# Hybrid decoder trunk on one core: operand sums emitted two FFN tiles early, four FFN weights split through a DMA, residual additions at the norm's priority

## The chip, the cores and the metric

One core of one Trainium2 chip runs the whole program. The metric is the device time of one execution in microseconds, here the median of three runs. A separate profiled execution gives the trace; its own time stands in the table below.

## The reference, cut to what matters

Two layers on 528 tokens (16 meta tokens and 512 of input) of width 1024, all float32. Each layer is a token mixer and a gated MLP, each behind an RMSNorm and with a plain residual add; a last RMSNorm follows. The change touches the MLP and the norms:

```python
def conv_glu_ffn(h, w_up, conv_w, conv_b, w_down):
    u = causal_dwconv(jnp.einsum('btd,df->btf', h, w_up), conv_w, conv_b)
    gate, val = jnp.split(u, 2, axis=-1)
    return jnp.einsum('btf,fd->btd', jax.nn.silu(gate) * val, w_down)
...
for l in range(DEPTH):
    h = h + hybrid_mixer(rmsnorm(h, norm_mix_g[l]), w_in[l], ...)
    h = h + conv_glu_ffn(rmsnorm(h, norm_ffn_g[l]), w_up[l], ..., w_down[l])
return rmsnorm(h, final_norm_g)[:, N_META:]
```

D_FF is 2816, so the MLP has 22 tiles of 128 hidden units, each with a gate and a value.

## The kernel before

**Products in three terms.** Every large float32 product is taken with operands split into a high part and a remainder: weight wh and wl, activation xh and xl. One 128x128 block is three matmuls: wh by xh, wh by xl, wl by xh (`product`, and `q` in `pair_products`). The activations lie transposed, features on the partitions and tokens on the columns; the 528 columns are worked in two halves of 264 (256 or 258 where the last layer drops the meta tokens).

**How a split is made.** `split` (L420 to L427) casts the high part on ScalarE (L421). The remainder is one subtraction on VectorE (L427), or, with `by_dma=True`, a negated copy on ScalarE (L424) and a DMA from the GpSimd queue that adds the source to it (L425). Before, the second way is used for the down-projection weights `rd` that are spread into the FFN tiles, and for the sums `th`, `tl`.

**Weights.** `raw_src` lists the weight tiles in the order of their use and `items` says how each is prepared: "p" is a split on VectorE, "q" a split through the DMA, "a" to "d" make the sums that a fast tile needs. `take` (where TensorE picks up an item) prepares three items ahead by `prep`. Weights land in three buffers `raw`, by DMAs from the SyncE queue, and the split parts in four buffers each of `wh` and `wl`. An up-projection tile is 128x1024.

**FFN tiles.** Tiles 0 to 3 and 21 are plain: gate and value, two halves each, 8 blocks of three matmuls a half (`up_pair`). Tiles 4 to 20 are fast (`up_fast`): gate and value share seven products of half the size in place of eight (`pair_products`), which needs sums and differences of blocks of the weights and of the normalised activations. In a fast tile the order on TensorE is: products on X_B11 and X_B21, then X_T1 and X_T2, two half products of the down projection of the four tiles before, X_B22 and X_T3, two more down halves, X_T4. Each of the seven is 12 matmuls, a half of the down projection too. T1 to T4 are the operand sums, made once a layer by `sum_pair(a)` for each of four pairs of feature blocks: two additions that put xh and xl together (L1049), four additions and subtractions (L1055 to L1060), and two splits by DMA into `th` and `tl`. A pair takes four work buffers `t`, and the buffers that hold its results are free again when the DMAs have read them. Tile u and convolution buffers come out of the same seven buffers `t` (`TM = 7`): four for an FFN tile. In the loop over `GROUPS` near the end of `layer`, `sum_pair` is emitted behind plain tiles 1, 2 and 3.

**Order of the work.** TensorE and the SyncE queue run in the order in which the code emits. VectorE, ScalarE and GpSimd are ordered when the program is built, by a list scheduler with a model of time: of what is ready there, the instruction emitted first goes first, and `tc.high_priority(n)` lets its block go as if it had been emitted n places earlier. Norm generators (`norm_rest`, `norm_split`) run under `URGENT['n']` = 400 from `tick`. The residual additions and squares of `resid_sq` (L979, and L437, L441, L442 in `norm_sq`) have no such priority before.

Of the kernel before, what the change touches and what calls it, by code (L numbers as in the profile page):

```python
# [13 lines left out]
ALU = mybir.AluOpType  # L14
# [5 lines left out]
KD = D // P  # L20
SEQ = 512
META = 16
T = SEQ + META
# [7 lines left out]
NFF = 22  # L31

GROUPS = ((0, 4), (4, 8), (8, 12), (12, 16), (16, 22))
FAST = range(4, 21)
DOWNS = ((), (2, 2, 2, 2), (2, 2, 2, 2), (2, 2, 2, 2), (2, 2, 2, 1, 1, 0))
TM = 7
Q0 = 12
MAXH = 2
# [5 lines left out]
URGENT = {'h': 400, 'r': 400, 'n': 400, 'f': 400}  # L44
# [49 lines left out]
def hybrid_trunk_kernel(ctx, tc, x, w_in, w_out, w_up, w_down, par, pre_in, lru_w, kon, msk, rope, out):  # L94
    nc = tc.nc
    V, S, G, PE = nc.vector, nc.scalar, nc.gpsimd, nc.tensor
# [23 lines left out]
    def half(tag="hs", bufs=4):  # L120
        return tpool.tile([P, 264], F32, tag=tag, name=nm(tag), bufs=bufs)
# [49 lines left out]
    hT = const.tile([P, KD, T], F32, tag="hT", name="hT")  # L171
# [28 lines left out]
    raw_src, items = [], []  # L200
# [4 lines left out]
        group[f"x{j}"], group[f"y{j}"], group[f"s{j}"] = [M_LX + j], [M_LY + j], [M_RG + j]  # L205
    orders = [[m for k in o.split() for m in group[k]] for o in (ORDER, ORDER1)]

    def plain(src, kn, ring="raw"):
        raw_src.append((src, kn, ring))
        items.append(("p" if ring == "raw" else "q", len(raw_src) - 1, kn))  # L210

    for l in range(DEPTH):
        for m in orders[l]:
            plain(w_in[l, m], KD)
        for m in range(KD):
            plain(w_out[l, m], KD)

        for g, (k0, k1) in enumerate(GROUPS):
            rows = iter(range(KD))
            for i, j in enumerate(range(k0, k1)):  # L220
                down = [next(rows) for _ in range(DOWNS[g][i] if g else 0)]
                if j in FAST:
                    raw_src.extend((w_up[l, r], KD, "raw") for r in (j, NFF + j))
                    ri = len(raw_src) - 2
                    items.extend((k, ri, KD) for k in "ab")
                    for q, m in enumerate(down):
                        plain(w_down[l, m, :, slice(*GROUPS[g - 1]), :], 4, "rd")
                        if q == 0:
                            items.append(("c", ri, KD))
                    if not down:  # L230
                        items.append(("c", ri, KD))
                    items.append(("d", ri, KD))
                else:
                    plain(w_up[l, j], KD)
                    plain(w_up[l, NFF + j], KD)
        for m in range(KD):
            plain(w_down[l, m, :, k0:k1, :], k1 - k0)
    raws, ready, sums = {}, {}, {}
# [193 lines left out]
    def norm_sq(k, t0, n, apart=False):  # L432

        if k == 0 or apart and k == KD - 1:
            a = half("acc", 3) if k == 0 else half("hs")
            accs.setdefault(t0, []).append(a)
            S.activation(a[:, 0:n], hT[:, k, t0:t0 + n], AF.Square)  # L437
            return
        a = accs[t0][0]
        sq = half("hs")  # L440
        S.activation(sq[:, 0:n], hT[:, k, t0:t0 + n], AF.Square)  # L441
        V.tensor_tensor(a[:, 0:n], a[:, 0:n], sq[:, 0:n], op=ALU.add)  # L442
# [52 lines left out]
    def whole(hi, lo):  # L495
        return lambda t0, n: (hi[:, t0:t0 + n], lo[:, t0:t0 + n])
# [406 lines left out]
    def layer(l):  # L903
# [72 lines left out]

        def resid_sq(m):
            def f(i, t0, n, ps):
                V.tensor_tensor(hT[:, m, t0:t0 + n], hT[:, m, t0:t0 + n], ps[:, 0:n], op=ALU.add)  # L979
                norm_sq(m, t0, n, t0 + n == T)  # L980
            return f

        def norm_next(blk, hi_):
# [6 lines left out]
        phase[0].release()  # L990
        phase[0], n_t[0] = tc.alloc_tile_pool(name=f"mlp{l}", bufs=1), TM
        c0 = META if lastl else 0
# [33 lines left out]
        def up_pair(j):  # L1026
            us = {}

            def ev(key, m):

                def f(i, t0, n, ps):
                    if key not in us:
                        us[key] = new_u()
                    u, c = us[key]
                    S.copy(u[:, 2 + t0:2 + t0 + n], ps[:, 0:n])
                    o = max(t0, c0)
                    tap(u, c, m, o, t0 + n, ps[:, o - t0:n])
                return f
            return [(None, ev("g", j), lambda: gate(j, us)), (None, ev("v", NFF + j), lambda: value(j, us))]
# [4 lines left out]
        def sum_pair(a):  # L1044

            y = []
            for k in (2 * a, 2 * a + 1):
                y.append(big())
                V.tensor_tensor(y[-1][:, 0:2 * hn], xh[:, k, h0:T].bitcast(F32), xl[:, k, h0:T].bitcast(F32), op=ALU.add)  # L1049
            (b11, b12), (b21, b22) = ((t[:, 0:hn], t[:, hn:2 * hn]) for t in y)  # L1050
            for i in (0, 2):
                t = big()
                p0, p1 = t[:, 0:hn], t[:, hn:2 * hn]
                if i == 0:
                    V.tensor_tensor(p0, b11, b12, op=ALU.subtract)  # L1055
                    V.scalar_tensor_tensor(p1, p0, -1.0, b22, op0=ALU.mult, op1=ALU.subtract)
                    t2 = p1
                else:
                    V.tensor_tensor(p0, b22, b12, op=ALU.subtract)
                    V.scalar_tensor_tensor(p1, t2, -1.0, b21, op0=ALU.mult, op1=ALU.subtract)  # L1060
                split(t[:, 0:2 * hn].rearrange("p (h t) -> p h t", t=hn), *(x[:, a, i:i + 2, 0:hn] for x in tsum),
                      by_dma=True)
# [7 lines left out]
        def up_fast(j, halves):  # L1070
            us = {k: new_u() for k in "gv"}
            ug, uv = (us[k][0][:, 2 + h0:2 + T] for k in "gv")

            def evac(what, ps):
                p = ps[:, 0:hn]
                if what == "c11":
                    S.copy(ug[:, 0:hn], p)
                elif what == "u":
                    S.copy(ug[:, hn:2 * hn], p)
                elif what == "q5":  # L1080
                    S.activation(uv[:, hn:2 * hn], p, AF.Copy, scale=-1.0)
                elif what == "c11b":
                    V.tensor_tensor(ug[:, 0:hn], ug[:, 0:hn], p, op=ALU.add)
                elif what == "c12":
                    V.tensor_tensor(ug[:, hn:2 * hn], ug[:, hn:2 * hn], p, op=ALU.add)  # L1085
                    u, c = us["g"]
                    tap(u, c, j, c0, T, u[:, 2 + c0:2 + T])
                    gate(j, us)
                elif what == "v":
                    V.tensor_tensor(uv[:, hn:2 * hn], uv[:, hn:2 * hn], p, op=ALU.subtract)  # L1090
                else:
                    S.activation(uv[:, 0:hn], p, AF.Copy, scale=-1.0)
                    u, c = us["v"]
                    tap(u, c, NFF + j, c0, T, u[:, 2 + c0:2 + T])
                    value(j, us)
            cut_at = (len(halves) + 1) // 2

            def between(i):
                for f in (halves[:cut_at], halves[cut_at:])[i]:
                    f()  # L1100
            pair_products(xs_fast, KD // 2, hn, evac, between)

        def down_halves(m, xs):

            w = []

            def f(t0, n):
                if not w:
                    w.append(take())
                ps = ps_mm.tile([P, 512], F32, tag="mm", name=nm("mm"))  # L1110
                product(w[0], xs, t0, n, range(len(xs)), ps, True, True)
                resid(m)(0, t0, n, ps)
            return [lambda t0=t0, n=n: f(t0, n) for t0, n in hd]

        for g, (k0, k1) in enumerate(GROUPS):
            rows = iter(range(KD))
            prev = [whole(*act[k]) for k in range(*GROUPS[g - 1])] if g else []
            for i, j in enumerate(range(k0, k1)):
                halves = [f for _ in range(DOWNS[g][i] if g else 0) for f in down_halves(next(rows), prev)]
                if j in FAST:  # L1120
                    up_fast(j, halves)
                else:
                    if j == 0:
                        run_units([u for i_ in range(2) for u in up_pair(i_)], xs_norm, hv, first=4)
                    elif j > 1:
                        run_units(up_pair(j), xs_norm, hv)
                    if j in (1, 2, 3):
                        for a in {1: (0,), 2: (1, 2), 3: (3,)}[j]:
                            sum_pair(a)

        def final(t0, n):
# [27 lines left out]
    with tc.manual_schedule(engines={mybir.EngineType.PE, mybir.EngineType.SP}):  # L1159
# [132 lines left out]
        for l in range(DEPTH):  # L1292
            layer(l)
# [106 lines left out]
```

## Time and profile before

| what | us |
|---|---|
| median of 3 runs | 1287.32 (1286.71 to 1287.97) |
| the profiled execution, its own time | 1288.41 |
| span of its trace | 1286.5 |
| TensorE busy / VectorE busy / ScalarE busy | 1258.5 / 988.6 / 752.0 |
| mean granted TensorE clock | 0.987 |

A row of the trace gives an engine, a line of the kernel, the operation and its tiles (out<-in, buffer numbers left out); "idle before" or the bracket at the end is the time that the engine stood before it and what ended that. The engines are PE (TensorE), DVE (VectorE), ACT (ScalarE), POOL (GpSimd) and SP (SyncE); a q behind a name is the queue of that engine. Times are counted from the start of the span.

### The profile page before, as it was taken

The page shows a single profiled execution, that of the slowest core. Times are in us where ns is not written, and L with a number is a line of the kernel's source. Part 1 is how long each engine was busy: PE and PEld are TensorE (multiplying, and loading weights), DVE is VectorE, ACT ScalarE, POOL GpSimd, SP SyncE. Part 2 cuts the span into 40 slices and gives each one's busy share as a digit, 9 for nine tenths or more (in the row PEclk, how much of TensorE's full clock was granted, in tenths as well). Part 3 has the DMA queues.
Part 4 walks back from the last instruction along what each step waited for, and adds up shares of the span by engine and source line. Part 5 has one row for each costly group of instructions (what it writes and reads, how often), then busy time and mean ns, then how long its engine had stood idle before and what let it go on. Part 6 is the DMA issues. An engine that isn't in the chain of part 4 may idle for free.

```text
span 1286.5 us, 25758 instructions
## 1 busy us (share of the span) xinstructions
PE 1258.5 (98%) x10244; PEld 1245.9 (97%) x10244; DVE 988.6 (77%) x1946; ACT 752.0 (58%) x1442; POOL 79.5 (6%) x179
## 2 busy tenths in 40 slices
PE   9999999999899999999999999999999999999997
PEld 8999999999899999999999999999989999999996
DVE  7987676468788888887588767764896888888865
ACT  6665555347666666666456645553684666666652
POOL 0000000001211111100000000000021111111000
PEclk8999999999899999999999999999998999999998
DMA  5322312324555445544232223122265555555422
GB/s 197 98 78 67 100 50 66 99 67 122 126 132 132 131 128 136 132 124 115 75 99 67 66 66 100 50 83 66 87 136 139 132 132 131 132 137 135 111 88 74
DMA packets 53240, 135.32 MB, mean 105 GB/s; under 512 B 5632, under 2 KB 12288, under 8 KB 53120
## 3 DMA queue, kind: packets, MB, share of 16 engines
q1 hardware_dynamic: 39424, 110.46, 27.5%
q0 software_dynamic: 12544, 21.06, 9.7%
q10 hardware_dynamic: 1152, 2.16, 0.5%
q8 instruction: 80, 1.31, 0.4%
q14 instruction: 40, 0.33, 0.1%
HBM read 110.51 MB, written 2.10 MB: 88 GB/s over the span
## 4 chain that ended last, share of the span: by engine, by line
PE 86%; DVE 6%; ACT 3%; DMA 3%; issue 1%; SPq 0%; POOL 0%; DVEq 0%; ACTq 0%; POOLq 0%
PE mm L130 63%; PE mx L130 23%; DMA tl<-t 2%; DVE t L1000 1%; PE mx L137 1%; DVE wl L427 1%; DVE t L567 1%; DVE t L1138 0%; DMA raw<-in_w_in_dram 0%; DVE sc L591 0%; ACT wh L421 0%; ACT th L421 0%; DMA mk<-in_msk_dram 0%; DVE t L870 0%; ACT sc L674 0%
## 5 line engine op out<-in xcount | busy, mean ns | idle before, releaser
L130 PE MATMUL mm<-xh,wh 128*128 128x264 f32 (+1 forms) x1424 | 417.9, 293 | 0.8 <-ACT xh L421 0.8
L130 PE MATMUL mm<-xl,wh 128*128 128x264 f32 (+1 forms) x1424 | 404.3, 284 | 0.7 <-DVE xl L427 0.3
L130 PE MATMUL mm<-xh,wl 128*128 128x264 f32 (+1 forms) x1424 | 403.4, 283 | 0.0
L130 PE MATMUL mm<-ah,wh 128*128 128x264 f32 (+2 forms) x960 | 273.2, 285 | 0.0
L130 PEld LDWEIGHTS mm<-xl,wh 128*128 128x128 f32 x1424 | 268.8, 189 | 3.7 <-issue 1.9
L130 PE MATMUL mm<-al,wh 128*128 128x264 f32 (+2 forms) x960 | 272.4, 284 | 0.0
L130 PE MATMUL mm<-ah,wl 128*128 128x264 f32 (+2 forms) x960 | 272.1, 283 | 0.0
L130 PEld LDWEIGHTS mm<-xh,wh 128*128 128x128 f32 x1424 | 268.5, 189 | 3.6 <-issue 2.0
L130 PEld LDWEIGHTS mm<-xh,wl 128*128 128x128 f32 x1424 | 268.6, 189 | 0.2 <-DVE wl L1195 0.2
L427 DVE TENSOR_TENSOR wl<-raw,wh 128x1024 fp32r<-128x1024 f32 (+2 forms) x168 | 182.5, 1088 | 82.2 <-ACT wh L421 81.7
L421 ACT CAST wh<-raw 128x1024 fp32r<-128x1024 f32 (+2 forms) x168 | 158.3, 942 | 149.2 <-PE mm L130 143.6
L130 PEld LDWEIGHTS mm<-ah,wh 128*128 128x128 f32 x960 | 182.0, 190 | 0.1
L130 PEld LDWEIGHTS mm<-al,wh 128*128 128x128 f32 x960 | 181.9, 189 | 0.1
L130 PEld LDWEIGHTS mm<-ah,wl 128*128 128x128 f32 x960 | 181.9, 189 | 0.0
L1000 DVE SCALAR_TENSOR_TENSOR t<-t,pr,t 128x528 f32<-128x528 f32 (+1 forms) x176 | 132.7, 757 | 11.1 <-ACT t L1005 5.1
L130 PE MATMUL mx<-th,wh 128*128 128x264 f32 (+1 forms) x408 | 117.2, 287 | 0.0
L130 PE MATMUL mx<-th,wl 128*128 128x264 f32 (+1 forms) x408 | 116.6, 286 | 0.0
L130 PE MATMUL mx<-tl,wh 128*128 128x264 f32 (+1 forms) x408 | 116.3, 285 | 0.0
L1005 ACT ACTIVATE t<-t,pr 128x528 f32<-128x528 f32 (+1 forms) x68 | 56.0, 823 | 58.5 <-DVE t L1085 56.5
L427 DVE TENSOR_TENSOR wl<-ss,wh 128x1024 fp32r<-128x1024 f32 x68 | 83.0, 1221 | 4.6 <-ACT wh L421 1.8
L425 POOL DMA_DIRECT2D wl<-rd x64 | 56.6, 884 | 448.6 <-ACT wl L424 384.4
L130 PEld LDWEIGHTS mx<-tl,wh 128*128 128x128 f32 x408 | 78.3, 192 | 0.0
(231 smaller groups left out, 2170.9 us busy)
## 6 DMA issues: line engine op xcount, KB each, us to landing
raw<-in_w_up_dram SPq DMA_DIRECT2D x88, 512.0 KB, 3.6
raw<-in_w_in_dram SPq DMA_DIRECT2D x52, 512.0 KB, 3.6
rd<-in_w_down_dram SPq DMA_DIRECT2D x64, 256.0 KB, 2.7
wl<-rd POOLq DMA_DIRECT2D x64, 256.0 KB, 3.6
raw<-in_w_out_dram SPq DMA_DIRECT2D x16, 512.0 KB, 3.5
raw<-in_w_down_dram SPq DMA_DIRECT2D x16, 384.0 KB, 3.1
hT<-in_x_dram SPq DMA_DIRECT2D x4, 528.0 KB, 5.4
t<-in_rope_dram ACTq DMA_DIRECT2D x8, 264.0 KB, 3.3
```

Of the source, the lines that this page charges most:

```text
L130: PE.matmul(o, a, b, start=start, stop=stop, **kw)
L137: PE.transpose(o, a, ident[0:n, 0:n])
L421: S.copy(hi, src)
L425: G.dma_start(lo, src, accum_op=ALU.add)
L427: V.tensor_tensor(lo, src, hi.bitcast(F32), op=ALU.subtract)
L567: V.tensor_tensor(o, a, b, op=ALU.mult)
L1000: V.scalar_tensor_tensor(c[:, 0:cn], u[:, i + c0:i + c0 + cn], pr[l][:, w + i:w + i + 1], c[:, 0:cn], op0=ALU.mult, op1=ALU.add)
L1005: S.activation(c[:, a - c0:b - c0], src, AF.Identity, bias=pr[l][:, C_FB + m:C_FB + m + 1], scale=pr[l][:, C_FW + 3 * m + 2:C_FW + 3 * m + 3])
```

## The change

Three edits. The gate and value weights of FFN tiles 2 and 3 are split through the DMA in place of VectorE. The four `sum_pair` calls come behind tiles 1 and 2, two behind each, in place of one, two and one behind tiles 1, 2 and 3. The residual addition, its square and the running sum of squares get the priority that the norm has.

```diff
+SENT = (2, 3)
...
-    def plain(src, kn, ring="raw"):
+    def plain(src, kn, ring="raw", by_dma=False):
         raw_src.append((src, kn, ring))
-        items.append(("p" if ring == "raw" else "q", len(raw_src) - 1, kn))
+        items.append(("q" if by_dma else "p", len(raw_src) - 1, kn))
...
-                        plain(w_down[l, m, :, slice(*GROUPS[g - 1]), :], 4, "rd")
+                        plain(w_down[l, m, :, slice(*GROUPS[g - 1]), :], 4, "rd", True)
...
-                    plain(w_up[l, j], KD)
-                    plain(w_up[l, NFF + j], KD)
+                    plain(w_up[l, j], KD, by_dma=j in SENT)
+                    plain(w_up[l, NFF + j], KD, by_dma=j in SENT)
...
         def resid_sq(m):
             def f(i, t0, n, ps):
-                V.tensor_tensor(hT[:, m, t0:t0 + n], hT[:, m, t0:t0 + n], ps[:, 0:n], op=ALU.add)
-                norm_sq(m, t0, n, t0 + n == T)
+                with tc.high_priority(URGENT['n']):
+                    V.tensor_tensor(hT[:, m, t0:t0 + n], hT[:, m, t0:t0 + n], ps[:, 0:n], op=ALU.add)
+                    norm_sq(m, t0, n, t0 + n == T)
...
-                    if j in (1, 2, 3):
-                        for a in {1: (0,), 2: (1, 2), 3: (3,)}[j]:
+                    if j in (1, 2):
+                        for a in {1: (0, 1), 2: (2, 3)}[j]:
                             sum_pair(a)
```

## Rows read from the trace of the kernel before

**Rows 1.** The page: busy us, share of the span and instructions of each engine.
```profile
PE 1258.5 (98%) x10244; PEld 1245.9 (97%) x10244; DVE 988.6 (77%) x1946; ACT 752.0 (58%) x1442; POOL 79.5 (6%) x179
```

**Rows 2.** What TensorE waited for in the whole span: us in total, times, longest.
```profile
PE mm L130 <- DMA tl<-t: 9.0, 2, 4.8
PE mm L130 <- ACT th L421: 2.5, 2, 1.5
PE mx L130 <- DVE acc L442: 2.0, 2, 1.2
```

**Rows 3.** Fast tiles 4, 5 (layers 0, 1): us; PE, PEld, DVE, ACT, POOL busy; PEclk; DMA.
```profile
324.19:348.34 24.15, 18.88 (x134) 18.46 (x133) 16.76 (x29) 14.12 (x26) 4.73 (x8) 0.86 0.60 133
348.34:364.38 16.04, 16.04 (x134) 16.04 (x133) 13.66 (x22) 10.03 (x16) 1.85 (x4) 1.00 0.50 132
957.23:982.47 25.24, 19.00 (x134) 18.59 (x133) 16.86 (x30) 14.33 (x26) 6.18 (x6) 0.80 0.64 128
982.47:998.20 15.73, 15.73 (x135) 15.73 (x133) 13.26 (x22) 9.96 (x16) 1.71 (x2) 1.00 0.50 135
```

**Rows 4.** The chain that ended last, layer 0, around tile 4: start, us, what.
```profile
330.23 3.75 DMA tl<-t
...
334.03 0.81 PE mm L130 x2
```

**Rows 5.** Busy time by stretch (columns as in rows 3): plain tiles before tile 4.
```profile
293.30:324.19 30.89, 30.89 (x258) 30.89 (x256) 30.41 (x48) 24.21 (x46) 4.64 (x9) 1.00 0.55 138
...
927.00:957.23 30.23, 30.23 (x255) 30.23 (x255) 29.75 (x48) 23.60 (x45) 5.23 (x5) 1.00 0.59 139
```

**Rows 6.** Groups by line and shape, 293.3 to 324.19 us, VectorE and ScalarE: busy us, mean ns.
```profile
L427 DVE TENSOR_TENSOR wl<-raw,wh 128x1024 fp32r<-128x1024 f32 x5 | 6.1, 1216 | 2.6 <-ACT wh L421 2.6
L1049 DVE TENSOR_TENSOR t<-xh,xl 128x528 f32<-128x528 f32 x6 | 4.1, 696 | 0.1
...
L1055 DVE TENSOR_TENSOR t<-t 128x264 f32<-128x264 f32 x3 | 1.3, 418 | 0.0
...
L421 ACT CAST wh<-raw 128x1024 fp32r<-128x1024 f32 x4 | 4.2, 1050 | 1.1 <-PE mm L130 1.1
```

**Rows 7.** VectorE in order of time, layer 0: start us, us, what.
```profile
322.91 0.41 DVE L1060 SCALAR_TENSOR_TENSOR t<-t,t 128x264 f32<-128x264 f32 x1
...
328.14 0.43 DVE L1056 SCALAR_TENSOR_TENSOR t<-t,t 128x264 f32<-128x264 f32 x1
...
331.61 0.70 DVE L427 TENSOR_TENSOR al<-t,ah 128x528 fp32r<-128x528 f32 x1
```

**Rows 8.** ScalarE in order of time, layer 0: start us, us, what.
```profile
292.25 1.05 ACT L421 CAST wh<-raw 128x1024 fp32r<-128x1024 f32 x1 [1.79 <-PE mm L130]
...
309.40 0.36 ACT L1035 COPY t<-mm 128x264 f32<-128x264 f32 x1
...
329.25 0.65 ACT L424 ACTIVATE tl<-t 128x528 fp32r<-128x528 f32 x1
```

**Rows 9.** DMA issues by line: 348 to 573 us, median us from issue to landing.
```profile
raw<-in_w_up_dram SPq DMA_DIRECT2D x28, 512.0 KB, 3.6
wl<-rd POOLq DMA_DIRECT2D x28, 256.0 KB, 3.4
rd<-in_w_down_dram SPq DMA_DIRECT2D x28, 256.0 KB, 2.7
```

**Rows 10.** What TensorE waited for, 640 to 660 us (the norm into layer 1).
```profile
PE mm L130 <- ACT xh L421: 0.8, 2, 0.5
PE mx L130 <- DVE acc L442: 0.8, 1, 0.8
PE mm L130 <- DVE xl L427: 0.3, 1, 0.3
```

**Rows 11.** VectorE in order of time, the same norm: the last residual addition.
```profile
652.10 0.42 DVE L979 TENSOR_TENSOR hT<-hT,mm 128x264 f32<-128x264 f32 x1
```

**Rows 12.** VectorE in order of time, layer 1: the last pair's first subtraction.
```profile
960.68 0.43 DVE L1055 TENSOR_TENSOR t<-t 128x258 f32<-128x258 f32 x1 [0.27 <-DMA tl<-t]
```

## The prediction, made before any run of the changed kernel

> **What bounds the kernel now.** The page comes first: TensorE is busy 98% of the span, VectorE 77%, ScalarE 58% [rows 1]. So only two things can make this kernel faster without fewer matmuls: TensorE's pauses, and stretches in which its clock is low. The view of waits names the pauses. Two waits of 9.0 us in all end with the DMA that lands the remainder of an operand sum (`tl`), two more of 2.5 us with the cast of its high part (`th`); the next cause in size is 2.0 us for the norm's sum of squares [rows 2]. The busy time by stretch shows what they cost. Fast tile 4 is the first that uses the sums, and it takes 24.15 us in layer 0 where tile 5, with the same work, takes 16.04: 8.11 more. In layer 1 it is 25.24 against 15.73: 9.51 more [rows 3]. Each excess has two parts. The engine stands 24.15 - 18.88 = 5.27 us (layer 1: 6.24), and it is busy 18.88 us on what takes 16.04 elsewhere, 2.84 us more (layer 1: 3.27). The second part is the clock: the granted mean is 0.86 and 0.80 in these stretches and 1.00 in tile 5, so behind the pause the engine ran for a while at 1.2 GHz in place of 2.4.
>
> Why the sum is late is read from the chain of waits: the DMA of 3.75 us issued at 330.23 lets TensorE go on at 334.03 [rows 4]. VectorE is the cause ahead of it. In the plain tiles before tile 4 it is busy 30.41 of 30.89 us, in layer 1 29.75 of 30.23 [rows 5]: the whole queue of convolutions, weight remainders and sums runs late, and the fourth pair of sums stands at its end.
>
> **The change, part by part.** *Four weight remainders leave VectorE.* One costs 1.216 us [rows 6], so 4 x 1.216 = 4.86 us a layer come out of the saturated stretch. In their place come four negated copies on ScalarE (as long as the cast of that shape, 1.05 us [rows 6], 4.2 us in all) and four GpSimd DMAs of 512 KB. ScalarE goes from 24.21 to 28.4 of 30.89 us [rows 5]: it fits, without much to spare.
>
> *The fourth pair of sums moves.* A pair is two additions of 0.70 and four instructions of 0.42, 3.06 us [rows 6]. The third and fourth now stand together behind tile 2, ahead of tile 3's convolutions. The third pair ended at 322.91 + 0.41 = 323.32 [rows 7]. The fourth put behind it adds 3.06, the weights take 4.86 off: it ends near 321.5, and its first half, for T1 and T2, two instructions sooner, near 320.7. Before, that half ended at 328.14 + 0.43 = 328.57 [rows 7] and had landed when TensorE went on at 334.03 [rows 4], 5.46 later: cast, negated copy (its end 329.25 + 0.65 = 329.90 [rows 8]), DMA. The same from 320.7 gives 326.2. TensorE wanted it at 334.03 less the wait of 4.2 and the 1.0 before it, some 328.8 (9.0 and 2.5 over both layers [rows 2]; layer 0 has the smaller of each). So the data is there 2.6 us early, and pause and slow clock go together: -8.11 and -9.51, -17.62 us. Layer 1 repeats the pattern with the same queue.
>
> *The first new DMA.* Tile 2's gate weight is new on a path that TensorE will soon need. Its buffer comes free and the cast starts at 292.25 [rows 8]; cast and negated copy end at 294.35; the DMA is issued 0.33 after (329.90 to 330.23 [rows 8, 4]). A 256 KB DMA of this kind lands 3.4 us after its issue, and the plain loads grow by 3.6 - 2.7 = 0.9 from 256 to 512 KB [rows 9]. I take 3.4 + 0.9 = 4.3, an estimate, since it is the nearest row for the step in size: landing at 299.0. The ends are 3.4 (nothing for the size) and 6.8 (twice). A matmul is 16.04 / 132 = 0.1215 us; tiles 2 and 3 are 192 of them, so tile 2 starts at 324.19 - 23.3 = 300.9. Cost 0; at the long end, with one evacuation of 0.36 [rows 8] ahead of the copy, 1.0 us a layer. The other three weights each have 2.9 us more: their buffers come free every 24 matmuls and are wanted every 48. The raw buffer is held until the DMA has landed, some 5 us longer, and SyncE's queue of later loads waits on that; those weights are wanted at tile 4, 20 us off. GpSimd's queue gets the four issues before the sums; they are over before the first sum is.
>
> *What is late next.* With the pause gone, the remainder of tile 3's activation is wanted: it ended at 331.61 + 0.70 = 332.3 [rows 7], less 4.86 is 327.4, and the first down half wants its fourth block at 324.19 + 4 x 1.46 + 9 x 0.1215 = 331.1. It holds, but ScalarE at nine tenths may hand tile 3 over late. For that, the weight above and buffer waits I allow 0.8 us a layer, between 0 and the 5 us of the second rival.
>
> *Residual additions first.* At the norm into layer 1 TensorE waits 0.8 us for the last sum of squares and 0.8 + 0.3 us for operands of the first half [rows 10]; the last residual addition stood until 652.10 behind the norm's splits [rows 11]. Moving it ahead can save up to all 1.9 us; it can also put up to six instructions of 0.42 (three additions, three running sums), 2.5 us, ahead of splits on which TensorE waits already. The two push against each other on one queue, so I take 0. At the other norms no TensorE wait ends on such a step except the last one, where the addition and square follow the last matmul anyway: 0.
>
> **The sum.** The trace's execution took 1288.41 us, 1.09 above the median of the runs shown. 1288.41 - 17.62 + 2 x 0.8 = 1272.4; less 1.09, **1271.3 us**, 1.2% faster.
>
> **The rivals.** *The second: part of the pause stays.* ScalarE becomes the late engine: if its 4.2 us all stand before the last sum's cast, the sum lands at 330.4, 1.6 us after it is wanted, and tile 3's evacuation slips by as much. With one such wait each for sum, activation and weight, 2 to 5 us a layer return, some of it as low clock: 1274 to 1280. For it: the 28.4 of 30.89. Against it: ScalarE now pauses in this stretch for VectorE, which gets lighter.
>
> *The third: the order does not change as emitted*, since the scheduler takes what it finds ready. Then only the 4.86 us count; the wait shrinks from 5.2 to 0.4, still near 1272. So either edit alone nearly closes the gap, which is why I hold "faster" to be safe, and no change to need two mishaps.
>
> *The fourth, slower: work buffers.* Pairs one and two now stand together ahead of tile 2's buffers: eight buffers out of seven, and those of the results are free only when their DMA lands. VectorE already stood 0.27 us for such a landing [rows 12]. Tile 2's first evacuation was at 309.40 [rows 8]; its PSUM bank, one of four, is wanted at 324.19 - 96 x 0.1215 = 312.5. If that evacuation must wait until the second pair has landed, after the first pair's chain of 5.46 and its own (309.4 + 2 x 5.46 = 320.3), TensorE stands 8 us, the clock falls again for 3, and 11 a layer against 8.8 saved gives 1293. It decides against the change when the evacuation slips by more than about 9 us.
>
> *The fifth: the DMA starves.* The DMA issued at 330.23 landed in 3.75 us [rows 4] while VectorE worked at its additions without a pause that the rows show, against 3.4 in the steady tiles [rows 9]. If GpSimd had to wait for a pause of VectorE, which has 0.48 us in 30.89 [rows 5], tile 2's weight would come some 30 us late: about 1350. The Trainium skill (GPSIMD Engine Reference, section Key points) says that GpSimd shares its SBUF interfaces with VectorE and contends with instructions that have two inputs there, which would be the ground for this. The 3.75 us speak against it.
>
> **How the numbers follow.** The forecast has 0.62, the second rival 0.23, the third 0.03 (faster too), the fourth 0.06, the fifth 0.01; 0.05 is for gains given back so nearly that nothing is seen. A difference under 0.2%, 2.6 us, cannot be told from none here. Faster 0.88, same 0.05, slower 0.07. The range starts at 1288.41 - 17.62 - 1.9 - 1.09, rounded to 1268, where nothing is late and the norm gains all, and reaches to 1279, into the second rival.
>
> **What would show it.** Right: in both layers tile 4 takes 16 to 17 us at a granted clock of 1.00; no TensorE wait ends on `tl`; eight fewer 128x1024 remainders of `raw` on VectorE; the fourth pair's additions before 324. Wrong: a wait on `wl` at tile 2's first matmuls, on PSUM at tile 3, a granted clock under 1 before tile 5, or waits in the norms of more than the 1.9 us.

## The result, and the profile after

The changed kernel takes 1302.13 us (1301.39 to 1303.88, 3 runs) against 1287.32: a ratio of 1.0118, with an interval of 1.0095 to 1.0141. It is 14.8 us slower where 16 us faster were forecast. Its profiled execution took 1301.39 us, with a span of 1299.6.

The waits of TensorE over the whole span answer to [rows 2]. The big wait on `tl` is down from 9.0 to 1.6 us. In its place stand one on a weight remainder split through the DMA and one on ScalarE's evacuations, neither of which the kernel before has:

```profile
PE mm L131 <- DMA wl<-raw: 8.7, 2, 4.4
PE mm L131 <- ACT t L1007: 7.3, 3, 3.3
PE mm L131 <- DMA tl<-t: 1.6, 1, 1.6
```

Where they stand is seen in the busy time by stretch: plain tiles 0 to 3 and fast tile 4 of layer 0, then of layer 1 (columns as in [rows 3]).

```profile
275.99:335.30 59.31, 51.63 (x400) 50.93 (x399) 39.08 (x75) 38.67 (x74) 10.22 (x20) 0.94 0.57 135
335.30:356.22 20.92, 18.43 (x134) 17.80 (x133) 16.05 (x25) 12.50 (x23) 2.69 (x5) 0.92 0.64 152
917.35:971.27 53.92, 49.42 (x401) 48.96 (x399) 32.94 (x64) 32.36 (x62) 8.36 (x8) 0.97 0.58 138
971.27:996.65 25.38, 19.42 (x134) 18.31 (x133) 21.86 (x37) 18.36 (x34) 6.58 (x6) 0.87 0.68 146
```

The same view of the kernel before gives the plain tiles without any pause:

```profile
276.06:324.19 48.13, 48.13 (x401) 48.06 (x399) 42.44 (x76) 33.27 (x67) 4.84 (x13) 1.00 0.46 122
...
909.98:957.23 47.25, 47.25 (x400) 47.20 (x399) 41.78 (x76) 32.69 (x66) 5.23 (x5) 1.00 0.48 122
```

The plain tiles cost 11.18 and 6.67 us more than before; in layer 0 that is 7.68 us of pauses and 3.5 us of slower clock (a granted mean of 0.94). Tile 4 gets 3.23 us back in layer 0 and nothing in layer 1 (+0.14). Together +14.8; the rest of the program is 1.7 us shorter, which makes the 13.1 us between the spans.

**How the first pause comes about.** Instructions in order of time, layer 0 of the changed kernel (start in us, length, engine, line, operation, tile, and in brackets the idle time before it and what ended it). First the weights' DMAs from GpSimd's queue, and the first DMA of a sum:

```profile
295.54 1.00 POOL L426 DMA_DIRECT2D wl<-raw  x1 [19.08 <-PE mm L131]
306.99 1.79 POOL L426 DMA_DIRECT2D wl<-raw  x2 [10.46 <-DVE t L1061]
309.52 0.86 POOL L426 DMA_DIRECT2D tl<-t  x1 [0.74 <-DVE al L428]
...
311.53 0.86 POOL L426 DMA_DIRECT2D wl<-raw  x1
```

The casts, the negated copies and an evacuation on ScalarE:

```profile
294.17 1.05 ACT L425 ACTIVATE wl<-raw 128x1024 fp32r<-128x1024 f32 x1
295.40 1.05 ACT L422 CAST wh<-raw 128x1024 fp32r<-128x1024 f32 x1 [0.17 <-PE mm L131]
...
304.14 1.05 ACT L422 CAST wh<-raw 128x1024 fp32r<-128x1024 f32 x1 [1.55 <-DMA raw<-in_w_up_dram]
...
305.64 1.99 ACT L425 ACTIVATE wl<-raw 128x1024 fp32r<-128x1024 f32 x2
...
320.73 1.04 ACT L422 CAST wh<-raw 128x1024 fp32r<-128x1024 f32 x1 [6.82 <-DMA raw<-in_w_up_dram]
321.68 1.03 ACT L1007 ACTIVATE t<-mm,pr 128x264 f32<-128x264 f32 x2
```

And the one long idle time of VectorE in this stretch:

```profile
321.81 1.23 DVE L428 TENSOR_TENSOR wl<-raw,wh 128x1024 fp32r<-128x1024 f32 x1 [10.27 <-ACT wh L422]
```

Tile 2's gate is cast at 292.48 and copied at 294.17, behind one evacuation. Tile 2's value is cast at 295.40, but its negated copy runs only at 305.64, together with that of tile 3's gate. In ScalarE's order other work stands between: evacuations, an activation and two casts of weights. 1.55 us of the 9.2 are a wait, for the weight of tile 3's value to land (the cast at 304.14); the rest is that other work. So the value's DMA is issued at 306.99, and TensorE stands 4.3 us for it from 307.38. The chain of waits shows where the late weight came from: SyncE issues its load only when the DMA of tile 2's gate has landed and its `raw` buffer is free.

```profile
295.54 4.80 DMA wl<-raw
...
300.39 3.72 DMA raw<-in_w_up_dram
...
304.14 0.02 ACT wh L422
```

**The second pause** comes from the next load behind a held buffer. Tile 4's gate is loaded into the buffer of tile 2's value, which is free only when the late DMA has landed: the load is issued at 311.68, before the change at 297.50. It takes 9.0 us to land, before 3.7, beside two DMAs of weights, four of sums and three other loads. ScalarE stands 6.82 us for the cast at 320.73 (tile 4's gate), and behind that cast stand the evacuations of tile 2 that TensorE needs for tile 3: it stands 3.3 us. VectorE, busy without a pause here before [rows 5], is idle for 10.27 us. SyncE's queue waited before too, as it runs ahead of the other engines, but for VectorE's subtractions. Its waits from 290 to 330 us (sum, count, longest, in us), first in the kernel before, then in the changed one:

```profile
SPq L249 <- DVE wl L427: 30.0, 5, 12.7
```

```profile
SPq L250 <- DMA wl<-raw: 36.9, 4, 18.5
```

The DMA issues from 293 to 335 us (KB each, median us to landing), against [rows 9]:

```profile
wl<-raw POOLq DMA_DIRECT2D x4, 512.0 KB, 5.6
raw<-in_w_up_dram SPq DMA_DIRECT2D x4, 512.0 KB, 7.3
tl<-t POOLq DMA_DIRECT2D x7, 264.0 KB, 6.9
rd<-in_w_down_dram SPq DMA_DIRECT2D x2, 256.0 KB, 11.0
```

At the median a plain load takes 7.3 us in place of 3.6, a sum's DMA 6.9. The first of the four weights' DMAs, alone, lands in 4.8 us and the slowest in 11.6; the load of tile 3's value, ahead of the crowd, takes 3.72. Layer 1 repeats the pattern: ScalarE stands 6.2 us for two late weights there (925 to 975 us).

### The profile page after: what moved, and what is told of

Same layout as the page of the kernel before. It is cut to its first block, busy times and chain, and to the rows that moved or that the text cites. A ratio compares the mean times of both kernels' runs of the same rounds, so it can differ in the third digit from the quotient of the medians.

```text
span 1299.6 us, 25769 instructions
## 1 busy us (share of the span) xinstructions
PE 1261.5 (97%) x10244; PEld 1247.8 (96%) x10244; DVE 980.6 (75%) x1938; ACT 758.7 (58%) x1450; POOL 86.3 (7%) x187
## 3 DMA queue, kind: packets, MB, share of 16 engines
q1 hardware_dynamic: 39424, 110.46, 27.0%
## 4 chain that ended last, share of the span: by engine, by line
PE 84%; DVE 6%; DMA 4%; ACT 3%; issue 1%; SPq 0%; DVEq 0%; ACTq 0%; POOLq 0%; POOL 0%
PE mm L131 61%; PE mx L131 22%; DMA tl<-t 2%; DMA raw<-in_w_up_dram 1%; PE mx L138 1%; DMA wl<-raw 1%; DVE wl L428 1%; DVE t L568 1%; DMA raw<-in_w_in_dram 0%; ACT wl L425 0%; DVE t L1140 0%; DVE sc L592 0%; ACT tl L425 0%; ACT th L422 0%; DVE hT L981 0%
## 5 line engine op out<-in xcount | busy, mean ns | idle before, releaser
L428 DVE TENSOR_TENSOR wl<-raw,wh 128x1024 fp32r<-128x1024 f32 (+2 forms) x160 | 172.6, 1081 | 78.5 <-ACT wh L422 78.1
L131 PEld LDWEIGHTS mx<-th,wh 128*128 128x128 f32 x408 | 77.6, 190 | 0.9 <-ACT t L1079 0.8
```

The lines of the kernel that those rows point to most:

```text
L131: PE.matmul(o, a, b, start=start, stop=stop, **kw)
L428: V.tensor_tensor(lo, src, hi.bitcast(F32), op=ALU.subtract)
```

## The experiments

Each run is compared with runs of the kernel before on the same chip; those had medians of 1287.2 to 1288.2 us. The texts of expectation were on record before the runs.

### The three edits one by one

Sums alone (from the changed kernel: no weight through the DMA, residual additions as before):

```diff
-SENT = (2, 3)
+SENT = ()
...
-                with tc.high_priority(URGENT['n']):
```

> Only the four sums move behind tiles 1 and 2; all eight weights are split on VectorE and the residual additions keep their place. Theory (the DMA split of tiles 2 and 3 is what lost the time: it holds the raw weight buffers until it has landed, so later weights come late and ScalarE's queue stands on their casts): no wait on a weight remainder at tile 2, the fourth sum lands some 3 us earlier than before, and 1272 to 1278 us. Rival (two pairs of sums standing together use up the work buffers, so tile 2's evacuation and with it TensorE at tile 3 wait): 1293 us or more, with a wait on PSUM at tile 3.

1285.39 us, ratio 0.9978 (0.9969 to 0.9987). The rival is out, but the gain is 2.4 us and not 10 to 15. Tile 4 of layer 0 takes 22.81 us; its pauses are now many:

```profile
PE mm L131 <- ACT t L1006: 1.3, 1, 1.3
PE mm L131 <- DMA tl<-t: 0.9, 1, 0.9
PE mx L131 <- ACT t L1078: 0.8, 1, 0.8
PE mm L131 <- DVE al L428: 0.4, 1, 0.4
PE mm L131 <- DVE wl L428: 0.3, 1, 0.3
```

The sum comes earlier, and what it overtook comes later: tile 3's evacuations, the sums of weights, tile 3's activation. The queue is as long as before and only its order differs.

The DMA split alone:

```diff
-                    if j in (1, 2):
-                        for a in {1: (0, 1), 2: (2, 3)}[j]:
+                    if j in (1, 2, 3):
+                        for a in {1: (0,), 2: (1, 2), 3: (3,)}[j]:
...
-                with tc.high_priority(URGENT['n']):
```

> Only the weights of tiles 2 and 3 go through the DMA; sums and residual additions as before. Theory (the DMA split lost the time): TensorE waits about 4 us a layer at tile 2's value weight and again behind it, 1298 to 1308 us. Rival (the work buffers of the sums lost it): VectorE lighter by 4.86 us a layer and 1270 to 1276 us.

1309.03 us, ratio 1.0161 (1.0144 to 1.0178), just above the range of the theory, and the rival is out: this edit is the loss, 21 us of it, and the early sums hide a part. Between 300 and 350 us TensorE waits for the weight, and then longer than before for the sums, though VectorE has less to do:

```profile
PE mm L131 <- DMA tl<-t: 6.6, 2, 3.6
PE mm L131 <- DMA wl<-raw: 4.1, 1, 4.1
PE mm L131 <- ACT th L422: 2.8, 1, 2.8
```

The residual additions alone (no split, sums in the old places), and then the change without the DMA split (the first line of this diff alone):

```diff
-SENT = (2, 3)
+SENT = ()
...
-                    if j in (1, 2):
-                        for a in {1: (0, 1), 2: (2, 3)}[j]:
+                    if j in (1, 2, 3):
+                        for a in {1: (0,), 2: (1, 2), 3: (3,)}[j]:
```

> Only the residual additions and squares get the norm's priority. Theory: within 2 us of before, 1285 to 1289 us, with the wait on the sum of squares at the norm into layer 1 gone and a longer wait on the normalised operands in its place. Rival (this edit is part of the loss): 1292 us or more.

> The whole change without the DMA split of tiles 2 and 3. Theory: as the sums alone, 1272 to 1278 us. Rival (sums or residual additions lost the time): 1293 us or more.

Residual additions: 1288.31 us, ratio 1.0002 (0.9992 to 1.0011), no difference. At the norm into layer 1 the wait on the sum of squares of [rows 10] is gone and that on the remainders is up from 0.3 to 1.0 us, as the two-sided bound had it:

```profile
PE mm L131 <- DVE xl L428: 1.0, 1, 1.0
PE mm L131 <- ACT xh L422: 0.8, 2, 0.5
```

Without the DMA split: 1285.61 us, ratio 0.9981 (0.9971 to 0.9990), the same as the sums alone. The rival is out, and the theory's 1272 to 1278 is missed again.

### What in the DMA split costs the time

Copies first: the weights' split is given the priority of the norm, so each negated copy follows its cast.

```diff
-                ready[i] = cut_in_two(r[:, 0:n], n, by_dma=kind == "q")
+                with tc.high_priority(400) if kind == "q" and kn == KD else nullcontext():
+                    ready[i] = cut_in_two(r[:, 0:n], n, by_dma=kind == "q")
```

> The changed kernel with the cast, the negated copy and the DMA of the four weights at a priority 400 places earlier, so that each negated copy stands right behind its cast on ScalarE. Theory (the loss comes mostly from the place of the negated copies: tile 2's value weight was copied 9 us after its cast, and everything behind it slid): tile 2's value remainder lands by about 306.5 us, no wait on a weight remainder, 1276 to 1290 us. Rival (the raw buffers held by the DMAs and the traffic itself are the loss, wherever the copy stands): tile 3's evacuation still waits behind a cast of a weight that has not landed, 1295 us or more.

1295.08 us, ratio 1.0051 (1.0037 to 1.0064), half of the loss back, outside the theory's range and at the edge of the rival's. The wait on a weight remainder is gone. In its place TensorE stands 5.6 us a layer at tile 3 for an evacuation, and the two rows of ScalarE say why:

```profile
PE mm L131 <- ACT t L1008: 11.1, 2, 5.6
```

```profile
305.55 1.05 ACT L423 CAST wh<-raw 128x1024 fp32r<-128x1024 f32 x1 [2.33 <-DMA raw<-in_w_up_dram]
...
317.86 0.57 ACT L1008 ACTIVATE t<-mm,pr 128x264 f32<-128x264 f32 x1 [4.41 <-DMA tl<-t]
```

It waits for the late weight again, and then 4.41 us for a work buffer `t` that a sum's DMA still reads. That DMA, issued at 310.73 with other DMAs in flight, took 7.1 us. This is the mechanism of the fourth rival; with the sums alone, at 1285.39 us, it cost nothing like that.

Then the split for one tile, and for one weight. Tiles: `SENT = (2,)` and `SENT = (3,)`; the runs with copies first have the edit above too. Single weights: `by_dma` stays on the gate's or the value's line alone, for the gate of tile 2:

```diff
-SENT = (2, 3)
+SENT = (2,)
...
-                    plain(w_up[l, NFF + j], KD, by_dma=j in SENT)
+                    plain(w_up[l, NFF + j], KD)
```

> The changed kernel with the DMA split for tile 2's two weights alone. Theory (a held raw buffer costs where the next loads into it are wanted soon: tile 2's buffers are loaded again for tile 3's value and tile 4's gate, whose casts stand in ScalarE's queue ahead of evacuations): most of the loss stays, a wait on tile 2's value remainder and one on PSUM at tile 3, 1292 to 1302 us. Rival (the loss is the traffic of four such DMAs beside the sums' DMAs): half of it goes, 1285 to 1291 us.

> The changed kernel with the DMA split for tile 3's two weights alone. Theory: their raw buffers are loaded again for tile 4's value and tile 5, wanted later, so no wait on a weight remainder and little on PSUM, 1281 to 1288 us. Rival (traffic of the DMAs): as with tile 2 alone, 1288 us or more.

> The DMA split for tile 2's weights alone, with the copies right behind the casts. Theory (two causes in tile 2: the value weight's late copy, and the raw buffers held until the DMAs land): the wait of 4.6 us on the value remainder goes, a wait on PSUM at tile 3 comes in its place, 1287 to 1292 us. Rival (the late copy is all of tile 2's cost): as without the split, 1284 to 1287 us.

> The DMA split for tile 2's gate alone, the one of the four whose DMA runs alone and whose copy was on time. Theory: its raw buffer is let go at about 300.3 us in place of 294.5, tile 3's value weight is cast late, but no wait on a weight remainder follows: 1283 to 1288 us. Rival (holding the first raw buffer is the root of the loss): 1290 us or more.

> The DMA split for tile 2's value alone, its copy right behind its cast. Theory (tile 2's cost needs both of its DMAs: the first holds the buffer that tile 3's value is loaded into, the second runs beside that load and slows it, so its cast blocks ScalarE): with one DMA the load is issued on time, and the time is within 2 us of no split, 1283 to 1288 us. Rival (the value weight's held buffer alone is the cost): 1289 us or more.

| weights through the DMA (sums and residual additions as in the change) | us | ratio to before |
|---|---|---|
| none | 1285.61 | 0.9981 (0.9971 to 0.9990) |
| tile 2, gate | 1285.19 | 0.9973 (0.9961 to 0.9985) |
| tile 2, value, copy first | 1287.89 | 1.0002 (0.9993 to 1.0012) |
| tile 2, both | 1292.40 | 1.0038 (1.0023 to 1.0053) |
| tile 2, both, copies first | 1291.86 | 1.0031 (1.0021 to 1.0042) |
| tile 3, both | 1285.94 | 0.9987 (0.9978 to 0.9996) |
| all four | 1302.13 | 1.0118 (1.0095 to 1.0141) |

All five times lie in the ranges of their theories, though not all their reasons hold. With tile 2 alone less than half of the loss stays (6.8 of 16.5 us), the wait on the remainder is there (4.6 us in layer 0) and the one at tile 3 is not; tile 2's value costs 2.3 us where the text had said within 2. Against no split, tile 3's two cost nothing and tile 2's two 6.8 us, so two such DMAs do not cost this much wherever they stand. (That tile 3's traffic is not free is seen below.) Tile 2's gate alone costs nothing, its value alone 2.3 us, both together 6.3 to 6.8, with the copies in either order: the late copy is not all of tile 2's cost. ScalarE's waits for a weight to land (290 to 335 us) follow the pattern. In the changed kernel:

```profile
ACT wh L422 <- DMA raw<-in_w_up_dram: 8.4, 2, 6.8
```

With both of tile 2 and copies first:

```profile
ACT wh L423 <- DMA raw<-in_w_up_dram: 2.2, 1, 2.2
```

With the gate of tile 2 alone:

```profile
ACT wh L422 <- DMA raw<-in_w_up_dram: 0.6, 1, 0.6
```

With no split, with tile 2's value alone and with tile 3's two there is none. So with two held buffers in a row, and their DMAs beside the next load, the load is late enough to stop ScalarE for 2.2 us; with one it is 0.6 us or nothing. That this wait is what makes the 6.3 us is argued from the pattern and not shown: with copies first most of the loss stands at tile 4, not in the plain tiles. Plain tiles and tile 4 of layer 0, first with no split, then with both of tile 2 and copies first (columns as in [rows 3]):

```profile
276.65:325.05 48.40, 48.35 (x400) 48.07 (x399) 41.94 (x77) 32.08 (x65) 5.75 (x13) 1.00 0.43 113
325.05:347.29 22.24, 19.03 (x134) 17.77 (x133) 17.82 (x28) 15.40 (x28) 3.81 (x8) 0.92 0.69 163
```

```profile
276.29:326.05 49.76, 48.63 (x400) 48.14 (x399) 37.20 (x70) 31.94 (x63) 5.72 (x12) 1.00 0.50 128
326.05:351.25 25.20, 20.26 (x134) 18.96 (x133) 20.15 (x33) 17.56 (x33) 5.58 (x10) 0.86 0.64 148
```

That all four cost 16.5 us where 6.8 and 0.3 are the parts was seen and not taken apart further. A fourth `raw` buffer, which would test the held buffers by themselves, was not tried.

### What the early sums leave, and a faster version

Sums in place (from the run with the sums alone): a pair overwrites its two first buffers and holds two `t` where it held four.

```diff
-                t = big()
...
+            V.tensor_tensor(b11, b11, b12, op=ALU.subtract)
+            V.tensor_tensor(b12, b22, b12, op=ALU.subtract)
+            V.scalar_tensor_tensor(b22, b11, -1.0, b22, op0=ALU.mult, op1=ALU.subtract)
+            V.scalar_tensor_tensor(b21, b22, -1.0, b21, op0=ALU.mult, op1=ALU.subtract)
```

> Sums behind tiles 1 and 2, all weights split on VectorE, residual additions as before, and each pair of sums computed in place in its two first buffers, so that a pair holds two work buffers in place of four. Theory (with the sums early, what is late is tile 3's evacuation and convolution, kept back by work buffers that wait for the sums' DMAs): VectorE no longer waits on a landing of a sum, TensorE's waits at tile 4 fall under 2 us a layer, 1272 to 1279 us. Rival (VectorE's work alone is too much for this stretch, in whatever order): within 2 us of the sums-only run, 1283 to 1287 us.

> The kernel before with the sums computed in place, in their old place behind tiles 1, 2 and 3. Theory (the place of the fourth pair sets its landing): the wait on the sum's DMA at tile 4 stays at 3 us or more a layer, 1283 to 1288 us. Rival (the buffers alone were the brake): 1279 us or less.

> The whole change with the negated copies first and the sums in place. Theory (VectorE relieved of 4.86 us a layer, buffers free, copies in time): 1269 to 1276 us. Rival (the DMA split costs more than VectorE's time is worth): slower than the run with the sums in place and no DMA split.

Early and in place: 1284.04 us, ratio 0.9974 (0.9963 to 0.9985), the rival's range: the work buffers that the sums hold are not what is left. In the old place: 1289.92, ratio 1.0017 (1.0008 to 1.0026), slower, with 5.3 us on `tl` in layer 0; both theories missed it from below. With all four weights through the DMA and copies first: 1293.94, ratio 1.0053 (1.0037 to 1.0068); the rival held.

> The DMA split for tile 3's weights alone, its copies first on ScalarE, and the sums in place: VectorE lighter by 2.4 us a layer at little cost. Theory: 1278 to 1285 us, not slower than the sums in place without any DMA split (1284.0). Rival (any DMA split in this stretch costs more than it saves): 1287 us or more.

> As the run before with tile 3's value weight alone, whose raw buffer VectorE let go only at 309.5 us in the kernel before, so that the DMA holds it no longer. Theory: the best of these, 1278 to 1284 us. Rival: 1287 us or more.

> The DMA split for tile 3's value alone with the sums as in the change, not in place. Theory (work buffers and VectorE's load each cost a part): between the sums in place (1281.3) and no DMA split (1285.6), 1281 to 1285 us. Rival (in place is worth nothing here): 1281 us or less.

Tile 3's two weights, copies first, sums in place: 1287.58 us, ratio 0.9995 (0.9986 to 1.0004), the rival. Tile 3's value alone: 1281.32, ratio 0.9948 (0.9931 to 0.9964), the theory. So the split of tile 3's gate costs 6.3 us here, and no weight is waited for on ScalarE in either run. What the traces show to differ is traffic, though its share of the 6.3 us is not isolated: the sums' DMAs from 300 to 320 us take up to 8.9 us to land with both weights and up to 4.7 with one, and VectorE waits for a work buffer that such a DMA reads (290 to 335 us), 0.6 us with one and with both:

```profile
DVE t L1052 <- DMA tl<-t: 3.7, 1, 3.7
```

Tile 3's value alone with the sums not in place: 1279.84, ratio 0.9934 (0.9918 to 0.9951), in the range of the rival, so the theory there fell; the intervals of the two forms overlap. The in-place run with tile 3's value alone has one wait of size left in layer 0 (300 to 345 us), on the fourth sum's DMA:

```profile
PE mx L131 <- DMA tl<-t: 2.2, 1, 2.2
```

So the last two runs take the fourth pair off the DMA, for two more subtractions on VectorE:

```diff
-                      by_dma=True)
+                      by_dma=a < KD // 2 - 1)
```

> The best so far (tile 3's value through the DMA, sums in place) with the fourth pair of sums split on VectorE in place of the DMA. Theory (what is left at tile 4 is the landing of the fourth pair's second half, 2.2 and 1.8 us, and the clock behind it): no wait on a sum's DMA, 1273 to 1279 us. Rival (VectorE's two more subtractions of 0.7 us delay tile 3's activation by as much): 1280 to 1284 us.

> Tile 3's value through the DMA with its copy first, the sums behind tiles 1 and 2 as in the change (not in place), the fourth pair split on VectorE. Theory (the in-place form cost 1.5 us with the DMA split of the fourth pair): 1273 to 1278 us, the fastest. Rival (with the fourth pair off the DMA the buffers of the in-place form count): 1278 us or more.

1277.01 us in place, ratio 0.9912 (0.9897 to 0.9927), and 1276.00 not in place, ratio 0.9910 (0.9893 to 0.9927): both in the ranges of their theories, no difference between the two forms, and both faster than the kernel before and the changed one. Tile 4 of layer 0 in the last run, busy time by stretch:

```profile
324.74:342.43 17.69, 16.57 (x134) 16.16 (x133) 16.54 (x27) 11.53 (x22) 1.95 (x5) 1.00 0.63 166
```

TensorE's longest waits there (300 to 345 us):

```profile
PE mm L131 <- DVE al L429: 0.6, 1, 0.6
PE mm L131 <- ACT ah L423: 0.5, 1, 0.5
```

No sum is waited for, the clock stays at 1.00 through tile 4, and the tile takes 17.69 us against 24.15 [rows 3]. What is left is tile 3's activation, which the forecast had named as late next. In layer 1 tile 4 takes 17.48 us against 25.24, but the plain tiles before it take 49.76 against 47.25, with a wait of 1.7 us for an evacuation:

```profile
903.56:953.32 49.76, 47.98 (x401) 47.52 (x399) 42.83 (x80) 35.84 (x72) 8.07 (x7) 1.00 0.52 125
953.32:970.80 17.48, 16.53 (x135) 15.92 (x134) 15.98 (x26) 11.14 (x20) 1.74 (x2) 1.00 0.65 161
```

## Why the prediction was wrong, point by point

**What bounds the kernel: right.** Pause and clock at tile 4 were the gap. The last run closes it but for 1.65 us in layer 0 (17.69 against 16.04) and 1.75 in layer 1 (17.48 against 15.73).

**The first new DMA: right.** Forecast to land at 299.0, it landed at 300.34 against a need at 300.9, with 0.6 us to spare in place of 1.9, and split alone that weight costs nothing. An evacuation stood ahead of the copy, and my 4.3 us for 512 KB was 4.8 alone.

**"The other three weights each have 2.9 us more": the step that failed.** It set buffer against need and took for granted that copy and DMA follow the cast. In ScalarE's order tile 2's value was copied 9 us after the cast was done (296.45 to 305.64), behind other work and a cast that waited 1.55 us for its weight: 4.3 us of pause in layer 0, 4.4 in layer 1. The sentence that GpSimd's four issues are over before the first sum falls with it: two came at 306.99 and the last at 311.53, between the sums' DMAs. The sum allowed 0.8 us a layer for late weights, buffer waits and a late tile 3; the plain tiles took 11.18 and 6.67 us more.

**"Those weights are wanted at tile 4, 20 us off": failed.** The first load behind a held buffer was tile 3's value, not tile 4's. Even for tile 4 the need on TensorE was the wrong measure. The cast has a place in ScalarE's order ahead of evacuations, and a late weight blocks those: 8.4 us of ScalarE's time in layer 0, the 3.3 us pause at tile 3, the 10.27 us of idle VectorE. Both pauses are among the signs of being wrong that the forecast had named, a wait on `wl` in tile 2 and one on PSUM at tile 3. I counted the later issue on SyncE's queue and did not ask what was queued behind the instruction that waits for it.

**The price of a DMA was taken from a quiet stretch.** With the last weights' DMAs, four of sums and the loads in flight together a weight's DMA took 11.6 us and the load of tile 4's gate 9.0.

**The moved sums: the size failed.** "The fourth put behind it adds 3.06, the weights take 4.86 off" counted VectorE's work and not the order it displaces. Alone it gains 2.4 us. The third rival ("either edit alone nearly closes the gap") falls with it: the one gains 2.4, the other loses 21.

**Residual additions: 0 forecast, 0 measured,** by the exchange of waits that was named.

**The second rival** named the engine that came late, ScalarE, but not the reason: in the plain tiles of layer 0 it was busy 38.67 of 59.31 us and stood 8.4 us for weights. Its 1274 to 1280 is out.

**The fourth rival,** slower by work buffers, had 0.06 and a price of 1293 (worked out from the profiled execution's 1288.41; from the median it is 1291.7). Its sign came true, but its wait is shown only once the copies stand first; in the changed kernel the weights come before it. **The fifth** is out: the first new DMA landed in 4.8 us, not in 30.

## What to carry to other kernels

Where work is moved to a DMA, ask when the DMA lets its source buffer go, which load waits for that buffer, and what stands behind the first consumer of that load on an engine that works in order, as ScalarE did with evacuations behind a late cast; the need on TensorE alone says too little. On a saturated engine a step that is moved forward pushes another one back, so count what it overtakes. The last version is 11 us faster where the change lost 15: some 2 us came with the sums behind tiles 1 and 2, 5.8 with the one weight whose buffer nobody wanted soon, 3.8 with the last sum taken off the DMA path.

## What was unexpected of the hardware

The DMA engines were full where the DMAs were slow, though the mean over the stretch hides it (152 GB/s from 293 to 335 us, 132 in the steady tiles). The packets that began between 308.70 and 327.50 us took 1.07 of the 16 engines' span, at 239 GB/s; before the change it was 0.67 at 139 in the same window. A load took 9.0 us there, 3.6 in the steady tiles, and a 264 KB accumulation up to 13.4, 3.4 at the median before.

```profile
308.70:327.50 18.80, 12.49 (x78) 12.28 (x79) 8.15 (x14) 9.32 (x18) 4.50 (x8) 0.82 1.07 239
```

An accumulating DMA also fills the engines for longer than a load of the same size. In the whole kernel before, GpSimd's queue (all accumulations) took 9.7% of the engines' time for 21.06 MB and SyncE's queue (nearly all loads) 27.5% for 110.46 MB. That is 1.85 times as much for each byte:

```profile
q1 hardware_dynamic: 39424, 110.46, 27.5%
q0 software_dynamic: 12544, 21.06, 9.7%
```
